# Banded attention's low key parts spread over two half-zero planes

## The chip, the cores and the metric

One core of a Trainium2 chip runs the whole program. The metric is the device time of one execution in microseconds: for the kernel before, 1607.87 us, the median of three runs (1607.34 to 1609.04). Lines L... are lines of the kernel before, unless the text says otherwise.

## What is computed

Two layers of an encoder over 512 tokens of width 1024: token mixing, cross-attention into 256 memory tokens, and a gated feed-forward part, each between two norms. The mixing joins three groups of heads and projects them; the change is in the third, eight query heads over two key heads with a band of 128 tokens to each side:

```
s = einsum(q, k) * scale - slope * |pos_q - pos_k|
s = where(|j - i| <= 128 and j valid, s, lowest float)
m = max(max(s), sink);  e = exp(s - m)
p = e / (sum(e) + exp(sink - m));  o = p @ v
```

A second group (latent attention) turns 32 of its query and key columns by sine and cosine of the position.

## The kernel before, in words

Products keep float32 accuracy by splitting an operand into a high part of a shorter type (`split`, L102, an ACT cast) and a low part (DVE, the difference). `mm3` (L147) then takes three products, L149 to L151; all projections go this way. Weights come by DMA into a stage of two buffers (`stage`, L106, issued by SP) and are split from there into `wh` and `wl` (`unit`, L114).

Each layer's `mix_phase` (L475) runs a list of attention units (four chunks of differential heads, then the banded heads in `swa_units`, L680, then the latent heads) as a software pipeline, and between its steps draws projections from `fill` (L854). Tiles wait for one another by their readers and writers; a scheduler sets the order on each engine from the program's order.

For the banded heads `in_swa_kv` (L512) writes keys into `KS`: plane 0 has the high parts of key head 0 in rows 0 to 63 and again in rows 64 to 127, plane 1 the same for key head 1, and plane 2 the low parts, key head 0 in the lower 64 rows and key head 1 in the upper 64 (L518, L519). `in_swa_q` (L533) writes queries into `SQ`: for key head b, the high part stands in the rows of b and the low part in the other 64. `score` (L682) takes two products for 128 queries against 256 or 384 keys: L692 over 128 rows gives high by high plus low by high, and L693 over the 64 rows of b alone gives high by low. L695 (DVE) then adds the masked distances `swd`. A layer has 32 such pairs.

`swd` is made once by POOL in `setup_rest` (L336 to L344) from the distances `dist0` and lies in its own buffer to the end. `glat` (L922), gains for the latent norm, has its own buffer too; L906 reads it, last in `in_av` (L499). `cos2` holds the cosine twice over, since L757 multiplies 32 columns at once. At the end of a layer `post_norm` and `pre_norm` make the next layer's input: POOL's L205 and L206 give a norm's factor, and POOL's L215 the first half of a row block times the gains.

Of the kernel before, what the change touches and what calls it, by code (L numbers as in the profile page):

```python
# [9 lines left out]
F32 = mybir.dt.float32  # L10
# [12 lines left out]
NT = 4  # L23
# [46 lines left out]
def encoder_kernel(  # L70
# [204 lines left out]
    neglam = cp.tile([P, DEPTH], F32, tag="neglam", name="neglam")  # L275
    dist_dram = dp.tile([P, NT, S], F32, tag="distd", name="dist_dram")
    dist0 = ap.tile([P, NT, S], F32, tag="dist", name="dist")
    swd = mp.tile([P, 1280], F32, tag="swd", name="swd")
    cos2 = cp.tile([P, NT, 32], F32, tag="cos2", name="cos2")
    sin2 = mp.tile([P, NT, 32], F32, tag="sin2", name="sin2")  # L280

    pr = tmp("e", (P, S), I32)
# [46 lines left out]
            nc.vector.scalar_tensor_tensor(out=dist0[:, t, :], in0=a, scalar=-1.0, in1=a, op0=ALU.mult, op1=ALU.max)  # L329
        nc.sync.dma_start(dist_dram, dist0)  # L330

    def setup_rest():
        for n in range(NT):
            c0, w = SWA_COLS[n]
            o = SWA_OFF[n]
            nc.gpsimd.tensor_copy(out=swd[:, o:o + w], in_=dist0[:, n, c0:c0 + w])  # L336
            if n > 0:
                v = swd[:, o:o + P]
                nc.gpsimd.affine_select(out=v, in_=v, pattern=[[1, P]], compare_op=ALU.is_ge, fill=MASKED,
                                        base=0, channel_multiplier=-1)  # L340
            if n < NT - 1:
                v = swd[:, o + w - P:o + w]
                nc.gpsimd.affine_select(out=v, in_=v, pattern=[[-1, P]], compare_op=ALU.is_ge, fill=MASKED,
                                        base=0, channel_multiplier=1)  # L344


        mf, mi = tmp("m", (P, 6, NT, 16)), tmp("m", (P, 4, NT, 16), I32)
        names = {}

        def rt(name, dt=F32):  # L350
            key = (name, dt == I32)
            names[key] = len([k for k in names if k[1] == key[1]])
            return (mi if dt == I32 else mf)[:, names[key]]

        inv = rt("inv")[:, 0, :]
        for k in range(16):
            nc.gpsimd.memset(inv[:, k:k + 1], ROPE_INV[k])
        pf = cp.tile([P, NT], F32, tag="pf", name="pf")
        nc.vector.tensor_copy(out=pf, in_=pc)
        ang, ki = rt("ang"), rt("ki", I32)  # L360
        for t in range(NT):
            nc.vector.tensor_scalar(out=ang[:, t, :], in0=inv, scalar1=pf[:, t:t + 1], scalar2=None, op0=ALU.mult)
        kf = rt("kf")
        nc.vector.tensor_scalar(out=kf, in0=ang, scalar1=1.0 / (2.0 * math.pi), scalar2=None, op0=ALU.mult)
        nc.vector.tensor_copy(out=ki, in_=kf)
        kp = []
        for j, (sh, mask) in enumerate(((0, 1023), (10, 1023), (20, None))):
            kj, kjf = rt(f"k{j}", I32), rt(f"kf{j}")
            src = ki
            if sh:  # L370
                nc.vector.tensor_scalar(out=kj, in0=ki, scalar1=sh, scalar2=None, op0=ALU.arith_shift_right)
                src = kj
            if mask is not None:
                nc.vector.tensor_scalar(out=kj, in0=src, scalar1=mask, scalar2=None, op0=ALU.bitwise_and)
            nc.vector.tensor_copy(out=kjf, in_=kj)
            kp.append((kjf, float(1 << sh)))
        for j, c in ((2, 0), (1, 0), (2, 1), (0, 0), (1, 1), (2, 2), (0, 1), (1, 2), (2, 3), (0, 2), (1, 3), (2, 4)):
            kjf, unit_ = kp[j]
            nc.vector.scalar_tensor_tensor(out=ang, in0=kjf, scalar=-unit_ * TWO_PI[c], in1=ang,
                                           op0=ALU.mult, op1=ALU.add)  # L380
        fix = kp[0][0]
        for op, s in ((ALU.is_gt, 1.0), (ALU.is_lt, -1.0)):
            for piece in (TWO_PI[0], TWO_PI[1] + TWO_PI[2]):
                if piece is TWO_PI[0]:
                    nc.vector.tensor_scalar(out=fix, in0=ang, scalar1=s * math.pi, scalar2=None, op0=op)
                nc.vector.scalar_tensor_tensor(out=ang, in0=fix, scalar=-s * piece, in1=ang,
                                               op0=ALU.mult, op1=ALU.add)
        nc.vector.tensor_scalar(out=ang, in0=ang, scalar1=PI, scalar2=-PI, op0=ALU.min, op1=ALU.max)
        cang = kp[1][0]
        nc.vector.scalar_tensor_tensor(out=cang, in0=ang, scalar=-1.0, in1=ang, op0=ALU.mult, op1=ALU.max)  # L390
        nc.vector.tensor_scalar(out=cang, in0=cang, scalar1=-1.0, scalar2=math.pi / 2.0, op0=ALU.mult, op1=ALU.add)
        nc.scalar.activation(sin2[:, :, 16:32], ang, AF.Sin)
        nc.scalar.activation(cos2[:, :, 0:16], cang, AF.Sin)
        nc.vector.tensor_copy(out=cos2[:, :, 16:32], in_=cos2[:, :, 0:16])
        nc.vector.tensor_scalar(out=sin2[:, :, 0:16], in0=sin2[:, :, 16:32], scalar1=-1.0, scalar2=None, op0=ALU.mult)


# [77 lines left out]
    def mix_phase(l, head):  # L475
# [9 lines left out]
        hT, latT, glat = head.hT, head.latT, head.glat  # L485
        kr = mp.tile([P, NT, 32], F32, tag="kr", name="kr")
        aV = slot("E", [P, NT, 2, 4, 64], F32R, "aV")
        KS_cV = slot("Sq", [P, 5, S], F32R, "KScV")
        KS, cV = KS_cV[:, 0:3, :], KS_cV[:, 3:5, :].rearrange("p a (k b d) -> p (a k) b d", b=4, d=64)
        SQ = [xp.tile([P, 2, S], F32R, tag=f"x{c}", name=f"SQ{c}") for c in range(4)]  # L490

        if l == 0:
# [19 lines left out]
        def in_swa_kv():  # L512
            st = stage(((0, 0, 0, rows(w, C_K, C_K + 256)),), KC, 256)
            ps = psum("mm")
            ws_chunk(ps, unit(st[:, :, 0:P]), hT, 0, S)
            nc.scalar.copy(KS[lo, 0, :], ps[lo])
            nc.scalar.copy(KS[up, 1, :], ps[up])
            nc.vector.tensor_tensor(out=KS[lo, 2, :], in0=ps[lo], in1=KS[lo, 0, :].bitcast(F32), op=ALU.subtract)  # L518
            nc.vector.tensor_tensor(out=KS[up, 2, :], in0=ps[up], in1=KS[up, 1, :].bitcast(F32), op=ALU.subtract)  # L519
            nc.scalar.copy(KS[up, 0, :], ps[lo])  # L520
            nc.scalar.copy(KS[lo, 1, :], ps[up])
            yield
            ps = psum("mm")
            ws_chunk(ps, unit(st[:, :, P:2 * P]), hT, 0, S)
            cvT = tmp("o")
            nc.scalar.copy(cvT, ps)
            pt = psum("at")
            for i in range(NT):
                nc.tensor.transpose(pt[:, i * P:(i + 1) * P], cvT[:, i * P:(i + 1) * P], ident)
            split_v(cV, pt.rearrange("p (k b d) -> p k b d", k=NT, d=64))  # L530
            yield
# [148 lines left out]
        def swa_units(cp_, ip, mdst):  # L680

            def score(u, a, bic):  # L682
                b, i, c = bic
                pr = slice(64 * b, 64 * (b + 1))
                c0, wd = SWA_COLS[i]
                o0 = SWA_OFF[i]
                h = c + 4 * b
                if a == 0:
                    u["nm"], u["sm"] = small(2, "snm"), small(2, "ssm")
                ps = psum("sc")  # L690
                q = SQ[c][:, b, i * P:(i + 1) * P]
                nc.tensor.matmul(ps[:, :wd], lhsT=q, rhs=KS[:, b, c0:c0 + wd], start=True, stop=False)  # L692
                nc.tensor.matmul(ps[:, :wd], lhsT=q[pr], rhs=KS[pr, 2, c0:c0 + wd], start=False, stop=True)  # L693
                e = u["e"][a] = tmp("e")
                nc.vector.tensor_tensor_reduce(  # L695
                    out=e[:, :wd], in0=ps[:, :wd], in1=swd[:, o0:o0 + wd], scale=SWA_SLOPES[h],
                    scalar=nsinks[:, l, h:h + 1], op0=ALU.add, op1=ALU.min, accum_out=u["nm"][:, a:a + 1])
# [33 lines left out]
        def mla_up(qT, kT, mV):  # L731
# [5 lines left out]
            def products(i):  # L737
                t0, t1 = i * P, (i + 1) * P
                psq, pskv = psum("mm"), psum("mm")
                for k in range(2):  # L740
# [13 lines left out]
                                        in1=sin2[:, i:i + 1, 0:16].to_broadcast([P, 5, 16]), op=ALU.mult)  # L754
                nc.vector.tensor_tensor(out=b5[:, :, 16:32], in0=r5[:, :, 0:16],
                                        in1=sin2[:, i:i + 1, 16:32].to_broadcast([P, 5, 16]), op=ALU.mult)
                nc.vector.tensor_tensor(out=r5, in0=r5, in1=cos2[:, i:i + 1, :].to_broadcast([P, 5, 32]), op=ALU.mult)  # L757
                nc.vector.tensor_tensor(out=qn[:, :, 64:96], in0=r5[:, 0:4, :], in1=b5[:, 0:4, :], op=ALU.add)
                nc.vector.tensor_tensor(out=kn[:, :, 64:96], in0=r5[:, 4:5, :].to_broadcast([P, 4, 32]),
                                        in1=b5[:, 4:5, :].to_broadcast([P, 4, 32]), op=ALU.add)  # L760
# [59 lines left out]
        if l == 0:  # L820
            with tc.issue_after(state["first"]):
                setup()
                setup_rest()
        run_all(av_gen)

        def seq(*gens):
            for g in gens:
# [89 lines left out]
    class Head:  # L917


        def __init__(self, l, hT):  # L920
            self.l, self.hT = l, hT
            glat = self.glat = mp.tile([P, 384], F32, tag="glat", name="glat")  # L922
            self.st = stage(((0, 0, 0, rows(w_in[l], B_CQ, B_CQ + 256)),), KC, 256)
            self.us = None
            nc.sync.dma_start(glat[:, 0:256], mla_q_norm_g[l:l + 1, :].to_broadcast([P, 256]))
            nc.sync.dma_start(glat[:, 256:384], mla_kv_norm_g[l:l + 1, :].to_broadcast([P, 128]))
            self.latT = slot("L", [P, 2, 3, S], F32R, "latT")
            self.ps, self.pend = {}, None
# [422 lines left out]
```

## Time and profile before

| what | value |
|---|---|
| median of three runs | 1607.87 us |
| the profiled execution, its own time | 1609.39 us |
| its span, first to last instruction | 1607.6 us |
| TensorE (PE) busy | 1564.0 us, 97% of the span |
| DVE, ACT, POOL busy | 984.1, 806.8, 119.6 us |
| granted TensorE clock, mean | 0.994 |
| DMA, mean | 104 GB/s |

PE stands for TensorE's products and PEld for its weight loads, which overlap them. A share of busy time is a mean over stages that have different limits, so the stage around the band is read by itself. Ends of products are modelled; distances between their starts are not, and those are used for prices.

### The profile page before, as it was taken

The page shows a single profiled execution, that of the slowest core. Times are in us where ns is not written, and L with a number is a line of the kernel's source. Part 1 is how long each engine was busy: PE and PEld are TensorE (multiplying, and loading weights), DVE is VectorE, ACT ScalarE, POOL GpSimd, SP SyncE. Part 2 cuts the span into 40 slices and gives each one's busy share as a digit, 9 for nine tenths or more (in the row PEclk, how much of TensorE's full clock was granted, in tenths as well). Part 3 has the DMA queues.
Part 4 walks back from the last instruction along what each step waited for, and adds up shares of the span by engine and source line. Part 5 has one row for each costly group of instructions (what it writes and reads, how often), then busy time and mean ns, then how long its engine had stood idle before and what let it go on. Part 6 is the DMA issues. An engine that isn't in the chain of part 4 may idle for free.

```text
span 1607.6 us, 21890 instructions
## 1 busy us (share of the span) xinstructions
PE 1564.0 (97%) x8225; PEld 1319.6 (82%) x8225; DVE 984.1 (61%) x1912; ACT 806.8 (50%) x1749; POOL 119.6 (7%) x208
## 2 busy tenths in 40 slices
PE   6999999899999999999999999998999999999998
PEld 6887877799888888888888878777998888888886
DVE  6898877666453544444566987857547535445544
ACT  4578878544554222232356787885446432322222
POOL 3100000300210000000130000003004000000000
PEclk9999999999999999999999999999999999999999
DMA  5532541232242323233235234512312432323221
GB/s 176 149 96 79 185 143 66 79 131 80 68 142 80 120 90 105 79 105 105 87 124 128 56 128 162 164 40 79 131 53 70 154 105 81 103 90 120 79 80 53
DMA packets 130011, 167.37 MB, mean 104 GB/s; under 512 B 21745, under 2 KB 100721, under 8 KB 129137
## 3 DMA queue, kind: packets, MB, share of 16 engines
q1 hardware_dynamic: 129904, 165.97, 32.2%
q8 instruction: 65, 1.06, 0.3%
q14 instruction: 42, 0.34, 0.1%
HBM read 150.22 MB, written 9.44 MB: 99 GB/s over the span
## 4 chain that ended last, share of the span: by engine, by line
PE 90%; DVE 3%; POOL 2%; ACT 2%; issue 1%; DMA 1%; SPq 0%; POOLq 0%; DVEq 0%; ACTq 0%
PE ps_mm L149 14%; PE ps_mm L151 14%; PE ps_mm L150 14%; PE ps_av L151 6%; PE ps_av L150 6%; PE ps_av L149 6%; PE ps_sc L151 5%; PE ps_sc L150 5%; PE ps_sc L149 5%; PE ps_at L404 3%; PE ps_av L575 2%; PE ps_av L576 2%; PE ps_sc L786 1%; PE ps_sc L693 1%; PE ps_at L182 1%
## 5 line engine op out<-in xcount | busy, mean ns | idle before, releaser
L104 DVE TENSOR_TENSOR wl<-st,wh 128x512 fp32r<-128x512 f32 (+1 forms) x406 | 279.4, 701 | 235.9 <-ACT wh L103 234.4
L103 ACT CAST wh<-st 128x512 fp32r<-128x512 f32 (+1 forms) x406 | 243.2, 616 | 291.5 <-PE ps_mm L150 130.2
L151 PE MATMUL ps_mm<-hfh,wl 128*128 128x512 f32 (+1 forms) x384 | 142.8, 372 | 2.3 <-DVE wl L104 2.3
L151 PE MATMUL ps_av<-hfh,wl 128*128 128x512 f32 (+1 forms) x384 | 142.8, 372 | 1.6 <-DVE wl L104 1.6
L150 PE MATMUL ps_mm<-hfl,wh 128*128 128x512 f32 (+1 forms) x384 | 143.0, 372 | 0.4 <-DVE hfl L104 0.4
L149 PE MATMUL ps_mm<-hfh,wh 128*128 128x512 f32 (+1 forms) x384 | 142.7, 372 | 0.6 <-ACT hfh L103 0.6
L149 PE MATMUL ps_av<-hfh,wh 128*128 128x512 f32 (+1 forms) x384 | 142.6, 372 | 0.0
L150 PE MATMUL ps_av<-hfl,wh 128*128 128x512 f32 (+1 forms) x384 | 142.6, 371 | 0.0
L149 PE MATMUL ps_sc<-dwh,f 128*128 128x512 f32 x320 | 124.7, 390 | 0.0
L150 PE MATMUL ps_sc<-dwl,f 128*128 128x512 f32 x320 | 124.5, 389 | 0.0
L151 PE MATMUL ps_sc<-dwh,f 128*128 128x512 f32 x320 | 124.5, 389 | 0.0
L103 ACT CAST dwh<-st 128x1024 fp32r<-128x1024 f32 x40 | 40.1, 1049 | 157.5 <-PE ps_sc L151 153.3
L104 DVE TENSOR_TENSOR pl<-ps_at,ph 128x512 fp32r<-128x512 f32 (+1 forms) x128 | 82.8, 654 | 24.7 <-ACT ph L103 23.7
L103 ACT CAST ph<-ps_at 128x512 fp32r<-128x512 f32 (+1 forms) x128 | 70.5, 562 | 29.8 <-PE ps_at L404 28.0
L151 PEld LDWEIGHTS ps_mm<-hfh,wl 128*128 128x128 f32 x384 | 72.3, 188 | 15.1 <-DVE wl L104 2.7
L151 PEld LDWEIGHTS ps_av<-hfh,wl 128*128 128x128 f32 x384 | 72.3, 188 | 14.3 <-DVE wl L104 2.0
L150 PEld LDWEIGHTS ps_mm<-hfl,wh 128*128 128x128 f32 x384 | 72.3, 188 | 13.9 <-DVE hfl L104 1.4
L149 PEld LDWEIGHTS ps_mm<-hfh,wh 128*128 128x128 f32 x384 | 72.3, 188 | 13.6 <-ACT hfh L103 1.1
L150 PEld LDWEIGHTS ps_av<-hfl,wh 128*128 128x128 f32 x384 | 72.3, 188 | 12.5
L149 PEld LDWEIGHTS ps_av<-hfh,wh 128*128 128x128 f32 x384 | 72.3, 188 | 12.5
L404 PE MATMUL ps_at<-ident,e 128*128 128x128 f32 x480 | 77.2, 275 | 3.3 <-DVE memTl L104 2.2
L205 POOL TENSOR_SCALAR rpost<-rpostss 128x1 f32<-128x1 f32 x24 | 9.0, 374 | 917.5 <-ACT hTh L201 703.5
(363 smaller groups left out, 3897.8 us busy)
## 6 DMA issues: line engine op xcount, KB each, us to landing
st<-in_w_ffn_in SPq DMA_DIRECT2D x44, 1024.0 KB, 4.9
st<-in_w_ffn_out SPq DMA_DIRECT2D x22, 1024.0 KB, 4.8
st<-in_w_xkv SPq DMA_DIRECT2D x16, 1024.0 KB, 5.3
st<-in_w_out SPq DMA_DIRECT2D x16, 512.0 KB, 4.8
st<-in_w_xq SPq DMA_DIRECT2D x8, 1024.0 KB, 5.1
st<-in_w_xo SPq DMA_DIRECT2D x8, 1024.0 KB, 5.0
st<-in_w_in SPq DMA_DIRECT2D x12, 512.0 KB, 3.9
q<-stg SPq DMA_DIRECT2D x48, 128.0 KB, 2.3
```

The source lines that it names most:

```text
L103: nc.scalar.copy(hi, src)
L104: nc.vector.tensor_tensor(out=lo, in0=src, in1=hi.bitcast(F32), op=ALU.subtract)
L149: nc.tensor.matmul(ps, lhsT=lh, rhs=rh, start=first, stop=False)
L150: nc.tensor.matmul(ps, lhsT=lh, rhs=rl, start=False, stop=False)
L151: nc.tensor.matmul(ps, lhsT=ll, rhs=rh, start=False, stop=last)
L182: nc.tensor.transpose(pt[:, c * P:(c + 1) * P], src_half[:, c * P:(c + 1) * P], ident)
L205: nc.gpsimd.tensor_scalar(out=r, in0=ms[:, 0:1], scalar1=ms[:, 1:2], scalar2=EPS, op0=ALU.add, op1=ALU.add)
L404: nc.tensor.transpose(pt[:, c * P:(c + 1) * P], e[:, k * P:(k + 1) * P], ident)
L575: nc.tensor.matmul(av, lhsT=v, rhs=hi, start=k == u["k0"], stop=False)
L576: nc.tensor.matmul(av, lhsT=v, rhs=lo, start=False, stop=k == u["k1"] - 1)
L693: nc.tensor.matmul(ps[:, :wd], lhsT=q[pr], rhs=KS[pr, 2, c0:c0 + wd], start=False, stop=True)
L786: nc.tensor.matmul(ps, lhsT=mla["qT"][:, h, i * P:(i + 1) * P], rhs=mla["kT"][:, h, :], start=True, stop=True)
```

## The change

The low parts of the keys move into two planes. Plane 2 has key head 0's in the lower 64 rows and zeros above, plane 3 has zeros below and key head 1's above; four memsets by POOL write the zeros (one for each half plane and layer). The second product runs over all 128 rows of the same query tile. The other edits make room for the fourth plane: the cosine is kept once and read twice by its access pattern, and `swd` and `glat` share one buffer (tag `gw`). For that, `banded` makes `swd` in the first layer after `in_av` has read `glat`, writes it to DRAM, and in the second layer loads it back.

```diff
-    swd = mp.tile([P, 1280], F32, tag="swd", name="swd")
-    cos2 = cp.tile([P, NT, 32], F32, tag="cos2", name="cos2")
+    swd_dram = dp.tile([P, 1280], F32, tag="swdd", name="swd_dram")
+    cos1 = cp.tile([P, NT, 16], F32, tag="cos1", name="cos1")
...
-    def setup_rest():
+    def banded():
+
+        swd = mp.tile([P, 1280], F32, tag="gw", name="swd")
+        if "swd" in state:
+            nc.sync.dma_start(swd, swd_dram)
+            return swd
+        state["swd"] = True
         for n in range(NT):
...
-
+        nc.sync.dma_start(swd_dram, swd)
+        return swd
+
+    def setup_rest():
...
-        nc.scalar.activation(cos2[:, :, 0:16], cang, AF.Sin)
-        nc.vector.tensor_copy(out=cos2[:, :, 16:32], in_=cos2[:, :, 0:16])
+        nc.scalar.activation(cos1, cang, AF.Sin)
...
-        KS_cV = slot("Sq", [P, 5, S], F32R, "KScV")
-        KS, cV = KS_cV[:, 0:3, :], KS_cV[:, 3:5, :].rearrange("p a (k b d) -> p (a k) b d", b=4, d=64)
+        KS_cV = slot("Sq", [P, 6, S], F32R, "KScV")
+        KS, cV = KS_cV[:, 0:4, :], KS_cV[:, 4:6, :].rearrange("p a (k b d) -> p (a k) b d", b=4, d=64)
...
-            nc.vector.tensor_tensor(out=KS[up, 2, :], in0=ps[up], in1=KS[up, 1, :].bitcast(F32), op=ALU.subtract)
+            nc.vector.tensor_tensor(out=KS[up, 3, :], in0=ps[up], in1=KS[up, 1, :].bitcast(F32), op=ALU.subtract)
+            nc.gpsimd.memset(KS[up, 2, :].bitcast(F32), 0.0)
+            nc.gpsimd.memset(KS[lo, 3, :].bitcast(F32), 0.0)
...
-                nc.tensor.matmul(ps[:, :wd], lhsT=q[pr], rhs=KS[pr, 2, c0:c0 + wd], start=False, stop=True)
+                nc.tensor.matmul(ps[:, :wd], lhsT=q, rhs=KS[:, 2 + b, c0:c0 + wd], start=False, stop=True)
...
-                nc.vector.tensor_tensor(out=r5, in0=r5, in1=cos2[:, i:i + 1, :].to_broadcast([P, 5, 32]), op=ALU.mult)
+                r5h = r5.rearrange("p h (a d) -> p h a d", a=2)
+                nc.vector.tensor_tensor(out=r5h, in0=r5h, in1=cos1[:, i:i + 1, :].unsqueeze(1).to_broadcast([P, 5, 2, 16]),
+                                        op=ALU.mult)
...
         run_all(av_gen)
+        swd = banded()
...
-            glat = self.glat = mp.tile([P, 384], F32, tag="glat", name="glat")
+            glat = self.glat = mp.tile([P, 384], F32, tag="gw", name="glat")
```

Line numbers grow by 7 to 12 in the changed kernel. The scheduler also moves rows. Three places matter below.

TensorE in layer 0, about the middle of the first banded units (ps_sc is a score's bank; L768, now L779, are transposes for the latent heads). Before:

```order
L692 MATMUL ps_sc<-KScV,SQ_555 128x256
L693 MATMUL ps_sc<-KScV,SQ_555 128x256
L692 MATMUL ps_sc<-KScV,SQ_554 128x384
L182 MATMUL ps_at<-ident,o 128x128 x4
L149 MATMUL ps_mm<-wh,latT 128x512
L150 MATMUL ps_mm<-wl,latT 128x512
L151 MATMUL ps_mm<-wh,latT 128x512
L693 MATMUL ps_sc<-KScV,SQ_554 128x384
```

Now:

```order
L701 MATMUL ps_sc<-KScV,SQ_555 128x256
L702 MATMUL ps_sc<-KScV,SQ_555 128x256
L701 MATMUL ps_sc<-KScV,SQ_554 128x384
L702 MATMUL ps_sc<-KScV,SQ_554 128x384
L149 MATMUL ps_mm<-wh,latT 128x384
```

The two products of a pair stand together, where other products stood between them; their number and their columns are the same.

SP's queue in layer 0, after the first differential head's copies (st is the weight stage, the 128x8x64 loads are the band's query weights, four for a pair of query heads; q_10 is a later differential head). Before:

```order
L330 DMA dist_dram<-dist 128x2048
L111 DMA st<-in_w_in 128x8x256
L111 DMA st<-in_w_in 128x8x64 x4
L466 DMA q_10_1002<-stg 32x2x512
L467 DMA q_10_1002<-stg 32x2x512
L468 DMA q_10_1002<-stg 32x1024
```

Now:

```order
L330 DMA dist_dram<-dist 128x2048
L111 DMA st<-in_w_in 128x8x256
L351 DMA swd_dram<-swd 128x1280
L111 DMA st<-in_w_in 128x8x64 x3
L474 DMA q_10_1003<-stg 32x2x512
L475 DMA q_10_1003<-stg 32x2x512
L476 DMA q_10_1003<-stg 32x1024
```

The write-out of swd stands ahead of the query weights' loads, and the fourth of these has gone behind the copies of q_10. In the second layer the reload of swd stands at the same place.

POOL between the layers, at the last row block of the layer's end (rpost and rpre are norm factors, lr that of the latent norm). Before:

```order
L205 TENSOR_SCALAR rpost<-rpostss 128x1
L206 TENSOR_TENSOR rpost<-rpost,neghalf 128x1
L215 TENSOR_TENSOR c<-x_3692,gains 128x512
L155 TENSOR_SCALAR lr<-lms 128x1
L156 TENSOR_TENSOR lr<-lr,neghalf 128x1
```

Now:

```order
L206 TENSOR_TENSOR rpost<-rpost,neghalf 128x1
L528 MEMSET KScV 64x512
L529 MEMSET KScV 64x512
L215 TENSOR_TENSOR c<-x_3695,gains 128x512
L155 TENSOR_SCALAR lr<-lms 128x1
```

The second layer's two memsets stand between the factor and L215. In the first layer one memset comes ahead of the identity matrix and one between L205 and L206 of the first row block.

## Rows read from the trace of the kernel before

**Rows 1.** The page's chain that ended last, shares of the span by engine.
```profile
PE 90%; DVE 3%; POOL 2%; ACT 2%; issue 1%; DMA 1%; SPq 0%; POOLq 0%; DVEq 0%; ACTq 0%
```

**Rows 2.** Busy time by stretches: stretch, its length, then each engine's busy us (instructions).
```profile
core 0: us, PE busy (x) PEld busy (x) DVE busy (x) ACT busy (x) POOL busy (x), PEclk, DMA share, GB/s
80.00:100.00 20.00, 20.00 (x107) 16.82 (x106) 19.60 (x52) 17.56 (x40) 0.00 (x0) 1.00 0.59 128
138.00:156.00 18.00, 15.03 (x84) 11.80 (x82) 14.84 (x44) 14.91 (x39) 0.88 (x2) 0.91 0.09 30
180.00:240.00 60.00, 60.00 (x338) 48.89 (x339) 43.90 (x128) 45.59 (x117) 0.00 (x0) 1.00 0.52 165
...
931.00:949.00 18.00, 15.23 (x83) 11.95 (x83) 15.43 (x46) 15.89 (x42) 0.89 (x2) 0.91 0.10 30
```

**Rows 3.** Line L693 in layer 0: count, ns min/median/max, first and last start, forms.
```profile
L693 PE MATMUL ps_sc<-KScV,SQ x32: 379/422/443, 130.7 to 239.4; 64*128 64x256 f32 x16, 64*128 64x384 f32 x16
```

**Rows 4.** TensorE in order of time: start us, us, operation, out<-in, weights, data; a 384-column pair.
```profile
161.29 0.28 PE L576 MATMUL ps_av<-pl,KScV 128*128 128x256 f32 x1
161.41 0.34 PE L692 MATMUL ps_sc<-KScV,SQ 128*128 128x384 f32 x1
161.67 0.44 PE L693 MATMUL ps_sc<-KScV,SQ 64*128 64x384 f32 x1
162.04 0.39 PE L151 MATMUL ps_mm<-memTh,wl 128*128 128x256 f32 x1
162.26 0.28 PE L149 MATMUL ps_mm<-memTh,wh 128*128 128x256 f32 x1
```

**Rows 5.** The same view, a 256-column pair.
```profile
189.06 0.28 PE L692 MATMUL ps_sc<-KScV,SQ 128*128 128x256 f32 x1
189.27 0.38 PE L693 MATMUL ps_sc<-KScV,SQ 64*128 64x256 f32 x1
189.58 0.39 PE L149 MATMUL ps_mm<-memTh,wh 128*128 128x256 f32 x1
```

**Rows 6.** The same view, 384-column products over 128 rows in sequence.
```profile
170.72 0.34 PE L150 MATMUL ps_mm<-wl,latT 128*128 128x384 f32 x1
170.90 0.34 PE L151 MATMUL ps_mm<-wh,latT 128*128 128x384 f32 x1
```

**Rows 7.** The same view, a product over 96 rows between two over 128.
```profile
108.42 0.40 PE L624 MATMUL ps_sc<-q 96*128 96x512 f32 x1
108.65 0.40 PE L151 MATMUL ps_mm<-hTh,wl 128*128 128x512 f32 x1
108.89 0.40 PE L149 MATMUL ps_mm<-hTh,wh 128*128 128x512 f32 x1
```

**Rows 8.** POOL and DVE in order of time: the start, and between the layers.
```profile
0.72 0.20 POOL masks.py:197 MEMSET ident<- 128x128 f32 x1 [0.29 <-POOLq L1340]
...
6.00 0.57 POOL L206 TENSOR_TENSOR rpre<-rpre,neghalf 128x1 f32<-128x1 f32 x1
...
10.06 1.42 DVE L218 SCALAR_TENSOR_TENSOR o<-x,rpre,gains 128x512 f32<-128x512 f32 x2 [10.06 <-DMA gains<-in_g_mix_pre]
...
819.78 0.98 POOL L206 TENSOR_TENSOR rpost<-rpost,neghalf 128x1 f32<-128x1 f32 x1
821.69 1.67 POOL L215 TENSOR_TENSOR c<-x,gains 128x512 f32<-128x512 f32 x1 [0.93 <-DVE x L234]
```

**Rows 9.** Layer 0: SP's loads, landing time, glat's last reader, ACT's cast, swd's copies.
```profile
55.12 12.56 SPq L111 DMA_DIRECT2D st<-in_w_in  x5
...
st<-in_w_in SPq DMA_DIRECT2D x8, 256.0 KB, 3.6
...
67.81 0.35 DVE L906 SCALAR_TENSOR_TENSOR m<-ps_mm,lr,glat 128x128 f32<-128x128 f32 x1 [1.26 <-POOL lr L156]
...
79.31 1.13 ACT L103 CAST wh<-st 128x512 fp32r<-128x512 f32 x2
...
L336 POOL COPY swd<-dist x4: 397/542/804, 32.5 to 48.4; 128x256 f32<-128x256 f32 x2, 128x384 f32<-128x384 f32 x2
```

More of the change, by code (lines that the diff above doesn't have):

```diff
@@ L683, in score @@
                 b, i, c = bic
-                pr = slice(64 * b, 64 * (b + 1))
                 c0, wd = SWA_COLS[i]
```

## The prediction

> **What bounds the kernel now.** I read the chain of waits first, then the busy time by stretches around the banded scores, then TensorE's instructions in order of time at single pairs of products. The chain [rows 1] is TensorE for 90% of the span, so a microsecond taken from TensorE's stream is worth close to a microsecond wherever TensorE is full. The stretches say where that is. The band's 32 pairs of a layer (L692 and L693) lie, in layer 0, between 130 and 240 us [rows 3]. From 180 to 240 us TensorE is busy 60.00 of 60 while ACT has 45.59 and DVE 43.90; from 138 to 156 us it is busy only 15.03 of 18, and the second layer has the same dip from 931 to 949 us (15.23 of 18) [rows 2]. In the dips softmax and evacuation on ACT and DVE set the pace; elsewhere in the band TensorE does.
>
> **What the second product costs.** Ends of matmuls are modelled, so I take distances between starts. Among products over 128 rows a 256-column one is followed 0.12 us later by the next (L576 at 161.29, L692 at 161.41) [rows 4], a 384-column one after 0.18 [rows 6]. At the pair three distances are longer. L692 with 384 columns to L693: 161.41 to 161.67, 0.26 where 0.18 is usual, so 0.08 too much. L693 to its follower: 161.67 to 162.04, 0.37 for 384 columns, 0.19 too much. And the follower itself, an ordinary 256-column L151: 162.04 to 162.26, 0.22 for 0.12, 0.10 too much. The sum is 0.37. The 256-column pair agrees: 189.06 to 189.27 is 0.21 and 189.27 to 189.58 is 0.31, again 0.09 and 0.19 over 0.12 [rows 5]; with 0.10 for the follower 0.38. I take 0.38.
>
> Is it the 64 rows? A product over fewer rows than 128 that still isn't slow is L624 over 96 rows: 512 columns take 0.23 (108.42 to 108.65), and its 512-column follower 0.24 (108.65 to 108.89) [rows 7]. So neither a short contraction nor a change of operand costs anything; what L693 has that L624 lacks is the 64-row form. The Trainium skill's page "TensorEngine Tiling (Array Packing)", section "Key Properties", says that a change of tiling mode drains the engine. By that rule the 64-row product pays on the way in and on the way out, and rows 4 agree.
>
> **The change, part by part.**
> - *Second product over 128 rows.* 64 pairs [rows 3] by 0.38 us = 24.3 us off TensorE's stream, if both products then follow one another as 128-row products do. The new columns are zeros and cost no extra time: a product streams the same 256 or 384 columns. Bounds: 0 (the price isn't the row form, below) and 24.3.
> - *What isn't kept.* Two dips of 18 us in two stretches of 109 us hold about a sixth of the pairs, 4.0 us; there TensorE's products lie on the chain only in part, and I count half lost: 2.0. In the full stretch 180 to 240 some 18 pairs lose 6.7 us, so ACT's 45.59 us stand in 53 (86%) and DVE's 43.90 (82%). From 80 to 100 us DVE is at 19.60 and ACT at 17.56 of 20 and TensorE still at 20.00 [rows 2], so these shares do not stop it by themselves; for new waits I take 10% of the other 20.3: 2.0. Both together could be 0 or, if ACT binds, half of everything (second rival).
> - *Memsets of the zero halves, two a layer, POOL.* One memset of 128 columns takes 0.20 us; four times the columns give some 0.55 each as a guess by columns, and the nearest POOL row of 512 columns, 1.67, is the upper end [rows 8]. At the program's start one comes ahead of rpre's power, but DVE's L218, which needs it, waits until 10.06 for the gains while that power began at 6.00: over 3 us of cover, so 0; without the cover it would be 0.55. Between the layers both stand ahead of L215, in front of which POOL idled 0.93 us (from 820.76 to 821.69) [rows 8]: 1.1 less 0.93 is 0.2 us, and TensorE's last transposes of that layer's input come out of that chain, so 0.2 counts. Bounds 0 and 2.4.
> - *The banded table.* Its ten POOL rows move behind the last reader of glat (L906 at 67.81 to 68.16). Each copy takes 0.40 to 0.80 [rows 9]; ten rows of 0.40 to 0.80 end between 72.2 and 76.2, I take 73.5. The table is first read past 130 us [rows 3], so POOL is covered. SP is not idle about it: the write-out to DRAM waits on POOL, and behind it stand three of the four loads for the band's first queries. They were all issued by 67.7 (55.12 plus 12.56); now the first two go out at about 74.0 to 75.0, landing in 3.6 us plus the 640 KB ahead of them (some 2.5 times 256 KB). ACT casts the first of these weights at 79.31 [rows 9]. That is a margin near zero: I count 0.3 us, bounds 0 and 5. The six copies of q that follow wait for stg themselves, whose cast stands on ACT just ahead of 79.31. The fourth load goes out behind them, but its cast has moved back as well: 0. In the second layer the reload waits for the same reader in the same place, with no POOL work before it: 0. Without the margin ACT stands and, behind it, the exponentials of the other heads.
> - *glat for the second layer* is loaded after the last banded score instead of early; its first reader is in the next layer: 0. *One cosine copy less* and the same 160 elements read by another pattern: 0 on a DVE that nobody waits for there.
> - *Reordered rows in layer 0.* The scheduler put the pairs together and moved some weight splits; I take 0, bounds minus 2 and plus 2.
>
> Sum: 24.3 - 2.0 - 2.0 - 0.2 - 0.3 = 19.8. The profiled execution took 1609.39, so 1589.6; the median of the runs shown (1607.87) is 1.5 below the profiled one, so **1588.1**.
>
> **Rivals.**
> - *ACT or DVE takes over.* The stretch 240 on and the dips could spread, so that half of the gain turns into waits on ph, pl and e: 12 us kept, 1609.4 - 12 - 1.5 = 1596. For it: the dips exist already. Against: TensorE full beside DVE at 98% [rows 2].
> - *The row form costs nothing.* The price would lie in two products into one bank with one stationary tile, and stay: 0.5 us of POOL and SP are left, 1608.4. Against it speak the .19 after L693, which has left the pair, and rows 7. The Trainium skill's page "TensorE: Matmul & The Clock Gate", section "Why this matters for your kernels", says that a product over 32 rows takes as long as one over 128. By that rule 64 rows would be no dearer than 128 and this would be the outcome; rows 4 show 0.37 for 0.18.
> - *SP is held.* If POOL's ten rows take 1.67 us each, as L215 does [rows 8], instead of at most 0.80, the table is done at 84.9, the loads land near 90, and ACT's cast is over 10 us late; the same delay in the second layer (the reload landing 10 us late) would eat all 19.8. That is the point from which it decides. At 12.5 us a layer: 1588.1 + 25 = 1613. Against: these very copies took 0.40 to 0.80, and the second layer has no POOL work in it.
>
> **How the numbers follow.** Forecast case 0.77, between 1582.5 (24.3 kept, 1 us from the order) and 1592; ACT or DVE takes over 0.14, 1592 to 1602; no gain 0.05; SP held 0.04. The range that leaves out no more than 2 in 10 is 1582 to 1600. About 0.2% (3.2 us) is what a measurement of this kernel can tell from no change; past it on the fast side lie the first two cases, 0.91; within it the third, 0.05; beyond it the fourth, 0.04.
>
> **What would show it.** Right: the second product's group reads 128x256 and 128x384 with about the first one's distances, L692 to L693 0.12 and 0.18 us, the follower 0.12 after 256 columns; the stretch from the first pair to the last shrinks from 109 us to near 99 in both layers, and the stages outside keep their lengths to 1 us. Wrong in size: TensorE's idle time grows in those stretches, with ACT's or DVE's evacuations as the releaser (the first rival). Wrong in cause: 0.3 between the starts of the pair stays. SP: ACT's cast of the band's query weights shows a wait on a transfer near 79 us, and the chain there names it. POOL: the gap ahead of L215 between the layers is filled, and TensorE's L182 wait there grows by more than 0.2 us.

## The result and the profile after

The changed kernel takes 1590.48 us in the median of four runs, before 1607.61 in the median of four: a ratio of 0.9892 with a 95% interval of 0.9879 to 0.9906, or 17.4 us saved (15.1 to 19.5). One of the four runs after took 2191.33 us at a mean granted clock of 0.656 and is left out of the ratio; the other three lie between 1589.46 and 1591.30, at 0.994 to 0.995, with 1589.66 in the middle. The forecast was 1588.1 within 1582 to 1600, so direction and range held; of the 19.8 us that the sum had, 17.4 came, 2.4 too few.

The page of the profiled execution after (1591.3 us, span 1589.5), busy time and chain:

```profile
PE 1543.9 (97%) x8225; PEld 1315.8 (83%) x8225; DVE 984.7 (62%) x1911; ACT 806.3 (51%) x1749; POOL 118.9 (7%) x212
...
PE 88%; DVE 4%; ACT 3%; POOL 3%; DMA 1%; issue 1%; SPq 0%; DVEq 0%; POOLq 0%; ACTq 0%
```

The chain was 90% TensorE before [rows 1]; it is 88% now, and DVE, ACT and POOL have one point more each. TensorE still sets the end. The line of the second product, now L702 (the first product of the pair is L701), in the view of one line:

```profile
L702 PE MATMUL ps_sc<-KScV,SQ x64: 278/331/427, 129.8 to 1009.1; 128*128 128x256 f32 x32, 128*128 128x384 f32 x32
```

Its median over both layers is 331 ns; L693 had 422 in layer 0 [rows 3] and 435 over both, with as many columns. The starts tell it better. TensorE in order of time, pairs of 384 columns:

```profile
178.84 0.42 PE L701 MATMUL ps_sc<-KScV,SQ 128*128 128x384 f32 x1
179.10 0.33 PE L702 MATMUL ps_sc<-KScV,SQ 128*128 128x384 f32 x1
179.27 0.28 PE L585 MATMUL ps_av<-ph,KScV 128*128 128x256 f32 x1
179.38 0.28 PE L586 MATMUL ps_av<-pl,KScV 128*128 128x256 f32 x1
179.50 0.28 PE L585 MATMUL ps_av<-ph,KScV 128*128 128x256 f32 x1
179.62 0.28 PE L586 MATMUL ps_av<-pl,KScV 128*128 128x256 f32 x1
179.74 0.34 PE L701 MATMUL ps_sc<-KScV,SQ 128*128 128x384 f32 x1
179.92 0.34 PE L702 MATMUL ps_sc<-KScV,SQ 128*128 128x384 f32 x1
```

The second pair stands behind ordinary products, as the pair of rows 4 did. L701 to L702 is 0.18 now, 0.26 before. From L702 to its follower it is 0.17 (179.10 to 179.27; 0.37 before), from that follower on 0.11 (0.22 before). The first pair stands behind two transposes, which cost 0.08 of their own ahead of L702. A pair of 256 columns answers to rows 5 in the same way:

```profile
191.86 0.28 PE L701 MATMUL ps_sc<-KScV,SQ 128*128 128x256 f32 x1
191.98 0.28 PE L702 MATMUL ps_sc<-KScV,SQ 128*128 128x256 f32 x1
192.10 0.40 PE L149 MATMUL ps_mm<-wh,memTh 128*128 128x512 f32 x1
192.33 0.40 PE L150 MATMUL ps_mm<-wl,memTh 128*128 128x512 f32 x1
```

0.12, 0.12 and then 0.23, the ordinary distance of 512 columns [rows 7]. The stretches after, with the first start of the second product at 129.8 and its last in layer 0 some 11 us earlier than before:

```profile
core 0: us, PE busy (x) PEld busy (x) DVE busy (x) ACT busy (x) POOL busy (x), PEclk, DMA share, GB/s
80.00:100.00 20.00, 20.00 (x108) 16.94 (x106) 19.20 (x51) 16.88 (x38) 0.00 (x0) 1.00 0.62 138
138.00:156.00 18.00, 14.31 (x95) 11.01 (x94) 16.79 (x50) 16.49 (x44) 0.86 (x2) 1.00 0.18 56
180.00:230.00 50.00, 49.98 (x307) 43.93 (x306) 40.13 (x120) 41.11 (x108) 0.00 (x0) 1.00 0.57 181
```

In the full stretch TensorE stays full (49.98 of 50) while ACT has risen to 82% and DVE to 80%; before they stood at 76% and 73% [rows 2]. The dip has got a little deeper: 14.31 of 18, for 14.95 in the 64-row run below at the same clock of 1.00; the 15.03 before stood at a clock of 0.91. From the first pair to the end of the last the band takes 99 us in layer 0 and 98 in layer 1, for 109 and 108 before.

POOL and the queues, in order of time: the memsets at the start and between the layers, the last load issues behind the table, and ACT's cast of the band's query weights.

```profile
5.93 0.52 POOL L529 MEMSET KScV<- 64x512 f32 x1
...
808.16 0.52 POOL L528 MEMSET KScV<- 64x512 f32 x1
808.74 0.52 POOL L529 MEMSET KScV<- 64x512 f32 x1
809.22 1.49 POOL L215 TENSOR_TENSOR c<-x,gains 128x512 f32<-128x512 f32 x1
```

```profile
72.27 2.94 SPq L111 DMA_DIRECT2D st<-in_w_in  x3
```

```profile
79.31 1.14 ACT L103 CAST wh<-st 128x512 fp32r<-128x512 f32 x2
```

The memsets take 0.52 each (estimated 0.55); L215 follows them with no gap and is itself 0.18 shorter than before [rows 8], so nothing is left of the 0.2 us. SP goes on at 72.27, and ACT's cast starts at 79.31, to the hundredth where it did [rows 9], without a wait: the 0.3 us were not spent either.

### The profile page after: what moved, and what is told of

Read it like the earlier page. It is cut to its first block, busy times and chain, and to the rows that moved or that the text cites. A ratio compares the mean times of both kernels' runs of the same rounds, so it can differ in the third digit from the quotient of the medians.

```text
span 1589.5 us, 21904 instructions
## 1 busy us (share of the span) xinstructions
PE 1543.9 (97%) x8225; PEld 1315.8 (83%) x8225; DVE 984.7 (62%) x1911; ACT 806.3 (51%) x1749; POOL 118.9 (7%) x212
## 4 chain that ended last, share of the span: by engine, by line
PE 88%; DVE 4%; ACT 3%; POOL 3%; DMA 1%; issue 1%; SPq 0%; DVEq 0%; POOLq 0%; ACTq 0%
PE ps_mm L151 14%; PE ps_mm L149 14%; PE ps_mm L150 14%; PE ps_av L151 6%; PE ps_av L150 6%; PE ps_av L149 6%; PE ps_sc L151 5%; PE ps_sc L150 5%; PE ps_sc L149 5%; PE ps_at L412 3%; PE ps_av L585 1%; PE ps_sc L797 1%; PE ps_av L586 1%; PE ps_at L182 1%; PE ps_sc L634 1%
## 5 line engine op out<-in xcount | busy, mean ns | idle before, releaser
L205 POOL TENSOR_SCALAR rpost<-rpostss 128x1 f32<-128x1 f32 x24 | 9.1, 379 | 917.7 <-ACT hTh L201 703.5
```

The source lines that it names most:

```text
L205: nc.gpsimd.tensor_scalar(out=r, in0=ms[:, 0:1], scalar1=ms[:, 1:2], scalar2=EPS, op0=ALU.add, op1=ALU.add)
```

## The experiments

Each run is compared with the kernel before on the same chip: the first four below with 1607.96 us, the next three with 1607.61, the last three with 1607.90.

**Is it the row form?** All else of the change stays: planes, memsets, table, order. Only the second product reads 64 rows again.

```
-nc.tensor.matmul(ps[:, :wd], lhsT=q, rhs=KS[:, 2 + b, c0:c0 + wd], ...)
+pr = slice(64 * b, 64 * (b + 1))
+nc.tensor.matmul(ps[:, :wd], lhsT=q[pr], rhs=KS[pr, 2 + b, c0:c0 + wd], ...)
```

> The changed kernel with one edit undone: the second product runs over the 64 rows of its key head again, on the new planes, in the changed kernel's order of work on every engine. Theory (the whole gain is the row form): the three distances of 0.21 or 0.26, 0.31 or 0.37 and 0.22 us come back at 64 places, and the time is that of the kernel before within 2 us, 1606 to 1610. Rival (the reordering, the shared buffer or the memsets brought part of it): between 1591 and 1603, by the part that they brought.

Measured: 1607.54 us, ratio 1.0 (0.9991 to 1.001). The whole gain is gone, so the row form carries all of it, and memsets, moved table and one cosine copy less are together worth nothing that shows. Every instruction of this run stands where it stands in the change, which makes it the best partner for a comparison of traces. The line of the product (L703 here):

```profile
L703 PE MATMUL ps_sc<-KScV,SQ x64: 379/435/687, 130.1 to 1029.7; 64*128 64x256 f32 x32, 64*128 64x384 f32 x32
```

I matched the two traces instruction by instruction (TensorE has 8225 products in each, in the same order) and added up by how much the distances between starts shrank. L701 to the second product: 2.97 us in layer 0 and 3.20 in layer 1. Second product to follower: 5.32 and 5.97. Follower to the next: 2.08 and 2.44. Together 22.0 us over 64 pairs, 0.34 each. So a pair costs the 0.38 that rows 4 and 5 gave, less what dips and waits hid. All other distances in the two bands grew by 1.40 and 0.73 us.

The weight loads show where the price sits. Before, about the pair of rows 4:

```profile
161.29 0.19 PEld L692 LDWEIGHTS ps_sc<-KScV,SQ 128*128 128x128 f32 x1
161.67 0.18 PEld L693 LDWEIGHTS ps_sc<-KScV,SQ 64*128 64x128 f32 x1 [0.19 <-issue]
162.04 0.19 PEld L151 LDWEIGHTS ps_mm<-memTh,wl 128*128 128x128 f32 x1 [0.19 <-DVE esink L708]
162.15 0.19 PEld L149 LDWEIGHTS ps_mm<-memTh,wh 128*128 128x128 f32 x1
```

After, about the pair at 191.86 above:

```profile
191.86 0.19 PEld L702 LDWEIGHTS ps_sc<-KScV,SQ 128*128 128x128 f32 x1
191.98 0.19 PEld L149 LDWEIGHTS ps_mm<-wh,memTh 128*128 128x128 f32 x1
```

After, the load of L702 starts 0.12 us ahead of its product (191.86 for 191.98), and so does its follower's. Before, the load of L693 starts with its product, at 161.67, and the follower's with the follower, at 162.04; the next is 0.11 ahead again (162.15 for 162.26). At all 64 pairs over 64 rows, in the kernel before and in this run, neither of these two loads starts more than 0.003 us ahead of its product. How much of the 0.38 these lost leads make up no run separates.

**A price of the change of form, or of every 64-row product?** The kernel before, each 64-row product cut into two of half the columns, so that two 64-row products follow one another at each visit.

```
-nc.tensor.matmul(ps[:, :wd], lhsT=q[pr], rhs=KS[pr, 2, c0:c0 + wd], ..., stop=True)
+for s0, s1 in ((0, wd // 2), (wd // 2, wd)):
+    nc.tensor.matmul(ps[:, s0:s1], lhsT=q[pr], rhs=KS[pr, 2, c0 + s0:c0 + s1], ..., stop=s1 == wd)
```

> The kernel before with each 64-row product cut into two 64-row products of half the columns (128 or 192), one right behind the other. Theory (the price is paid at the change of form, in and out): the pair of halves costs one way in and one way out, so the first half follows L692 after 0.21 to 0.26 as now, the second half follows the first after its columns alone (about 0.06 to 0.10), and the whole is 1607 to 1614 us. Rival (each 64-row product pays about 0.19 us by itself): 64 times 0.19 more, near 1620.

Measured: 1608.99 us, ratio 1.0009 (1.0 to 1.0019): 1.4 us by the ratio for 64 more products of 64 rows. Both halves together take 0.36 us (256 columns) or 0.40 (384) to the follower, one whole product 0.31 or 0.37. The second half starts 0.16 or 0.19 after the first, not the 0.06 to 0.10 of the theory, but from it to the follower it is only 0.20. In the median its load starts 0.06 ahead of it, while the loads of the first half and of the follower start with their products. So nearly all of the price hangs on going into the form and out of it; a further product inside costs 0.05 or 0.03. Some 370 of TensorE's products stand elsewhere than in the kernel before, so these distances say more than the time.

**The same cut over 128 rows**, as a control.

```
-nc.tensor.matmul(ps[:, :wd], lhsT=q, rhs=KS[:, 2 + b, c0:c0 + wd], ..., stop=True)
+for s0, s1 in ((0, wd // 2), (wd // 2, wd)):
+    nc.tensor.matmul(ps[:, s0:s1], lhsT=q, rhs=KS[:, 2 + b, c0 + s0:c0 + s1], ..., stop=s1 == wd)
```

> Control for the one before: the changed kernel with each second product cut into two 128-row products of half the columns. Theory: the extra instruction costs at most its weight load, distances of 0.06 to 0.10 us for a half; 1590 to 1594. If a cut product costs more than that at 128 rows too, the excess in the run before has to be read less this one's.

Measured: 1602.53 us, ratio 0.9961 (0.9948 to 0.9975), some 12 us above the change. The theory missed it. Its trace, a 256-column pair on TensorE and the weight loads about it (the halves are one row, x2):

```profile
185.64 0.28 PE L701 MATMUL ps_sc<-KScV,SQ 128*128 128x256 f32 x1
185.76 0.34 PE L703 MATMUL ps_sc<-KScV,SQ 128*128 128x128 f32 x2
185.94 0.33 PE L149 MATMUL ps_mm<-memTh,wh 128*128 128x256 f32 x1
186.10 0.28 PE L150 MATMUL ps_mm<-memTl,wh 128*128 128x256 f32 x1
```

```profile
185.52 0.19 PEld L701 LDWEIGHTS ps_sc<-KScV,SQ 128*128 128x128 f32 x1
185.64 0.31 PEld L703 LDWEIGHTS ps_sc<-KScV,SQ 128*128 128x128 f32 x2
185.87 0.19 PEld L149 LDWEIGHTS ps_mm<-memTh,wh 128*128 128x128 f32 x1
185.99 0.19 PEld L150 LDWEIGHTS ps_mm<-memTl,wh 128*128 128x128 f32 x1
```

In these rows loads start some 0.12 us apart, for a whole product and for a half, and products of 256 columns start 0.12 apart too. A half of 128 columns brings a load of its own, so I read the loads as what sets the distance here; no run shows that by itself. From 185.64 to the follower it is 0.30 for 0.24, and the follower then takes 0.16 for 0.12: 0.10 a pair. Pairs of 384 columns lose 0.05 at most in the median, so 64 pairs lose some 5 us. The Trainium skill's page "TensorE: Matmul & The Clock Gate", section "LDWEIGHTS (loading the stationary operand)", gives a load a time by its columns alone, whatever the rows. An estimate from its formula is 107 ns for 128 columns; the 0.12 between these rows is near it. The page of this run has TensorE busy 1549.6 us, 5.7 more than the change, which is about those 5. But the span grew by 12.0, so some 6.3 us more were idle: the added products also moved some 370 of TensorE's 8225 other products to other places. How much of the 6.3 is that order I did not separate, so the control is a poor one.

**64 rows, or fewer than 128?** The change, with head 0's product over 96 rows; what is dropped are rows whose keys are zero.

```
+n = P if b else 96
-nc.tensor.matmul(ps[:, :wd], lhsT=q, rhs=KS[:, 2 + b, c0:c0 + wd], ...)
+nc.tensor.matmul(ps[:, :wd], lhsT=q[:n], rhs=KS[:n, 2 + b, c0:c0 + wd], ...)
```

> The changed kernel with key head 0's second product over 96 rows (64 of low parts and 32 of zeros), key head 1's over 128, order of work unchanged. Theory (only the 64-row form is dear): 96 rows behave as 128, distances 0.12 and 0.18, time 1589 to 1592. Rival (any count below 128 is dear): half of the pairs pay 0.38 again, 12 us, near 1602.

Measured: 1591.13 us, ratio 0.9898 (0.9878 to 0.9917), the change's own time. A 96-row product among 128-row ones is free, as rows 7 had said.

**What gave time back in layer 1?** Against the 64-row run the profiled execution of the change is 20.9 us ahead at the end of layer 1's band, and 16.8 some 20 us later. In that place, ACT and TensorE in order of time and the stretch:

```profile
1022.26 0.62 ACT L103 CAST q<-st 128x512 fp32r<-128x512 f32 x1 [2.68 <-DMA st<-in_w_xq]
```

```profile
1024.14 0.39 PE L585 MATMUL ps_av<-ph,mV 128*128 128x256 f32 x1 [2.15 <-ACT ph L103]
```

```profile
1009.00:1039.00 30.00, 27.45 (x133) 19.26 (x133) 22.78 (x51) 26.07 (x61) 0.00 (x0) 0.94 0.37 129
```

ACT stands at a cast whose weights are still being loaded, with the last heads' work queued behind it, TensorE then stands for ACT, and the granted clock falls. The load was not issued late: it went out 20.9 us earlier than in the 64-row run (at 1013.63 for 1034.50), by as much as the band's end had moved. But it took 8.6 us to land, where it took 5.7 there. My theory was that this wait is the price of being early. Two kernels were made against it. In the first, POOL splits this half of w_xq:

```
-split(t[:, 0, k:k + 4, :], t[:, 1, k:k + 4, :], st[:, k:k + 4, 0:P])
+hi, src = t[:, 0, k:k + 4, :], st[:, k:k + 4, 0:P]
+nc.gpsimd.tensor_copy(out=hi, in_=src)
+nc.gpsimd.tensor_tensor(out=t[:, 1, k:k + 4, :], in0=src, in1=hi.bitcast(F32), op=ALU.subtract)
```

> The change, with the splitting of the first half of w_xq (one copy and one subtraction in two pieces per layer) moved from ScalarE and VectorE to GpSimd. In the changed kernel's trace ScalarE stood 2.68 us at that copy in layer 1, with the work of the last heads queued behind it, TensorE then waited 2.15 us for ScalarE, and 3.0 us of the gain were gone within six microseconds. Theory (the copy's wait for its load is what gave those 3.0 us back): GpSimd waits in its place, nobody stands behind it, and the time is 1587.0 to 1588.5. Rival (the 3.0 us are lost there anyway, by the clock or by ScalarE's load of work): 1590 to 1591. Second rival (GpSimd's copies end too late for the first product that reads them): over 1592.

Measured: 1589.51 us, ratio 0.9888 (0.9873 to 0.9903): 1 us above the theory's upper bound, 0.5 below the rival's lower one. In its trace the loss in that place is gone (TensorE is busy 29.86 us of 1009 to 1039) although the load took 7.2 us to land, but against the 1589.46 to 1591.30 of the change the time does not tell. In the second kernel the 1 MB load is cut in two:

```
-st = stage(((0, 0, 0, rows(w_xq[l], 0, 256)),), KC, 256)
+st = stage(((0, 0, 0, rows(w_xq[l], 0, P)), (0, 0, P, rows(w_xq[l], P, 256))), KC, 256)
```

> The change, with the load of w_xq for the first heads, 1 MB in one transfer of 8.6 us, cut into two transfers of 512 KB, the half that the copy reads first. Theory (the copy waits for the load): the first half lands some 2 to 4 us earlier, ScalarE's wait at the copy falls from 2.68 us to under 1, and the time is 1587.5 to 1589.5. Rival (the wait is not for this load's length, or the two transfers share the queues with the loads ahead and end together): 1590 to 1591.

Measured: 1591.14 us, ratio 0.9895 (0.9882 to 0.9909). ACT's wait was 1.86 us, and the two pieces took 6.1 and 7.1 us to land. The time lies just past the rival's upper bound and not in the theory's range. But the change itself has a wait of 2.68 us in one execution and of 1.41 in another (below), so whether the cut shortened the wait at all is not shown.

**One layer at a time.** The second product over 128 rows in layer 0 alone:

```
+pr = slice(64 * b, 64 * (b + 1)) if l else slice(0, P)
+nc.tensor.matmul(ps[:, :wd], lhsT=q[pr], rhs=KS[pr, 2 + b, c0:c0 + wd], ...)
```

> The change, with the second product over 64 rows in layer 1 alone (128 in layer 0); every instruction stands where it stands in the change. Theory (32 changes of row form at 0.38 us go in layer 0, less what the start of the trace adds; what layer 1 gains is a smaller sum because 3.0 us are given back behind it): layer 0 alone is worth the 12.7 us that the traces show at 460 to 918 us, so 1594 to 1596, and layer 1 the remaining 4 to 5. Rival (both layers are worth the same 8.5 us in the end): 1598.5 to 1599.5.

Measured: 1596.79 us, ratio 0.9934 (0.9921 to 0.9947), so layer 0 alone is worth 10.7 us (8.5 to 12.7); between the two expectations and nearer to the theory's 1596. Then layer 1 alone (`if not l`), and beside it the change once more and the split on POOL once more:

> The counterpart of the run with 64 rows in layer 1: the second product over 64 rows in layer 0 alone, 128 in layer 1, every instruction in its place as in the change. Theory (TensorE's busy time in the two bands falls by about 10 us each, and layer 1 gives 3.0 back at the copy that waits for w_xq): layer 1 alone is worth 6 to 7 us, so 1600.5 to 1602, and its trace shows ScalarE waiting over 2 us at the copy. Rival (the layers are worth the same, and the wait is chance): 1598.5 to 1599.5.

Measured: 1598.31 us, ratio 0.9939 (0.9925 to 0.9953), so layer 1 alone is worth 9.8 us (7.6 to 12.1). The theory's 1600.5 to 1602 fell; the rival's equal shares came within 0.2 us. ACT waits 1.21 us at the cast here, not over 2. A layer is worth about 10 us, and no fixed 3 us come off the second. The two alone sum to 20.5 and the change has 17 to 18; the intervals are too wide to say that they do not add up.

> The change itself once more, beside the run with the split on GpSimd on the same chip, so that a difference of one or two microseconds can be read. Both theories: 1589 to 1592.

Measured: 1590.26 us, ratio 0.9888 (0.9874 to 0.9901), runs from 1589.38 to 1590.87. The same rows of this second profiled execution of the same code, ACT, TensorE and the stretch:

```profile
1022.99 0.62 ACT L103 CAST q<-st 128x512 fp32r<-128x512 f32 x1 [1.41 <-DMA st<-in_w_xq]
```

```profile
1024.87 0.39 PE L585 MATMUL ps_av<-ph,mV 128*128 128x256 f32 x1 [0.88 <-ACT ph L103]
```

```profile
140.00:152.00 12.00, 9.27 (x54) 7.65 (x53) 10.49 (x30) 10.80 (x28) 0.86 (x2) 0.86 0.14 48
...
1009.00:1039.00 30.00, 28.81 (x152) 20.29 (x151) 25.20 (x56) 28.39 (x66) 0.00 (x0) 1.00 0.45 149
```

The load landed in 7.1 us this time, the wait is half as long, the clock stays at 1.00, and 1.4 us are given back (18.6 us ahead of the 64-row run, then 17.2) instead of 4.0. So most of what the first trace seemed to show was one execution's chance. In the profiles in which it is one transfer, this load lands in 5.6 to 8.6 us; what decides it I did not find.

> The change with the split of w_xq's first half on GpSimd, once more. Theory (the wait of ScalarE costs 3 us of time, and moving it gives them back for good): 2 to 4 us under the change in the same call. Rival (what is gained there is lost later, or to the longer work on GpSimd): within 1 us of the change.

Measured: 1588.33 us, ratio 0.9878 (0.9864 to 0.9891), runs from 1588.06 to 1589.45: 1.9 us under the change taken beside it, just below the theory's 2 and outside the rival's 1. Its trace has POOL wait instead, and the stretch full:

```profile
1020.05 1.17 POOL L864 CAST q<-st 128x512 fp32r<-128x512 f32 x2 [76.41 <-DMA st<-in_w_xq]
1021.18 2.53 POOL L865 TENSOR_TENSOR q<-st,q 128x512 fp32r<-128x512 f32 x2
```

```profile
1009.00:1039.00 30.00, 29.87 (x154) 20.62 (x152) 24.20 (x55) 29.15 (x69) 3.66 (x4) 1.00 0.44 144
```

TensorE has 29.87 of 30 busy for 28.81 of the change's own second execution: 1.1 us of the 1.9 lie here. But the load also landed in 5.6 us this time. The eight runs of this kernel have a mean of 1589.0 us, the seven others of the change one of 1590.2, some 1.2 us apart, with the kernel before within 0.3 us in all three groups. It is the fastest of the kernels run, though the intervals of the two ratios overlap.

## Why the prediction was right, and where it was off

- **Price of a pair, 64 × 0.38 = 24.3.** Right in cause and nearly in size. The three distances came out as predicted (0.18 or 0.12, the same again, 0.12 for the follower). In place, 22.0 us left TensorE's stream, where the sum had 24.3 less 2.0 for the dips, 22.3. The run over 64 rows shows the form to be the whole cause, the one with two products shows nearly all of it to be paid per visit, and the one over 96 rows that shortness alone is free. The "row form costs nothing" rival is out; the rule of the Trainium skill's "TensorEngine Tiling (Array Packing)", "Key Properties", that a change of mode drains the engine, fits, with a price beside it: 0.08 to 0.09 on the way in, and 0.19 and 0.10 behind it. That a drain is what costs is not shown; the rows show that the two weight loads at the change of form do not start ahead of their products.
- **New waits, 2.0.** About right: all other distances in the bands grew by 2.1 us (1.40 and 0.73). TensorE's idle time there explains 1.25 of it (3.05 us in the 64-row run to 3.85 in layer 0, 2.76 to 3.21 in layer 1); the rest is spread over rows. The rival in which ACT or DVE takes over did not come: TensorE stayed full from 180 to 230 us.
- **POOL 0.2 and SP 0.3.** Both were 0. Gap and shorter L215 took in the memsets, and ACT's cast did not move. The rival in which SP is held had its deciding point at 84.9 us; SP went on at 72.27.
- **Not in the sum: the copy of w_xq behind layer 1's band.** It stood in nobody's row, because before it was on time within 0.75 us. The bands shrank from 109 and 108 us to 99 and 98, as forecast; the 0 given to everything outside them was the term that failed: against the 64-row run, 4.2 us net were lost outside them in one execution (4.0 right behind layer 1's band) and 1.7 in the other (1.4 there). How much of the 2.4 us of error this is stays open. The split on POOL, which takes the wait away from ACT, was 1.9 us faster beside the change and some 1.2 by all runs of both. The first execution lost a further 1.2 us near 1095 us, where its clock was 0.77 (1085 to 1100); the second, at 0.89 there, did not.
- **Traces of one execution.** The sum was made on one profiled execution and its clock. From 140 to 152 us the granted clock had 0.86 in the profile before, 1.00 in that of the change, 0.86 in the change's second one. By matched rows, the second execution loses 1.7 us against the first from 129 to 152 us: 1.1 in a wait for ACT at 137.78 that the first does not have, and 0.6 in the stretch of the lower clock. At 800 us the first is 3.0 us ahead of the second, at the end 1.6 behind it. A stage's gain read from one pair of traces is uncertain by that much: it made the first layer look worth 12.7 us and the second 4 to 5. The run of layer 1 alone (9.8, 7.6 to 12.1) refuted the second figure; the first lies at the edge of the interval of layer 0 alone (8.5 to 12.7).

## What to carry to other kernels

A product over 64 rows among products over 128 pays for each visit, some 0.38 us here for its three distances, and little more when two products stand in it; filling the other 64 rows with zeros costs memsets that hide and no time on TensorE. Look for row forms of 64 in a stream where TensorE is full, and leave 96 alone. When a stage gets 10 us shorter, look at the loads that are issued near its end: where a copy on a busy engine waits for one, a slow landing holds up the work queued behind it, and an idle engine can wait in its place.

## What was not expected of the hardware

- The weight load of a 64-row product among 128-row ones starts with its product, and so does that of the product behind it, while a load ahead of a product over 128 or 96 rows in the same place starts some 0.12 us before it in the median.
- Cutting a 256-column product into two over 128 rows costs 0.10 us a pair, although as many columns stream; each half has a weight load of its own, and in the rows shown the loads start some 0.12 us apart. The same cut inside the 64-row form cost 0.05, and 0.03 for 384 columns; why it costs less there is not shown.
- TensorE is idle for 1.7 to 3.0 us in all between 140 and 152 us of the program, in several pieces. In eight of twelve profiles the granted clock of 140 to 152 us was 1.00, which is 2.4 GHz throughout; in four (before, layer 0 alone, 96 rows, the change again) it was 0.72 or 0.86, a mean with 1.2 GHz for a part. The change itself is on both sides, once each, and the execution with the lower clock loses 0.6 us more in that stretch. What decides it I did not find.
